# A decoder trunk: twelve output tiles of the mixer's projection by seven block products, memory's mean square in the first projections, and a triangle added behind the low keys

## The chip, the cores and the metric

The kernel runs on one core of one Trainium2 chip. The metric is the device time of one execution in microseconds, compared as a median over several runs. One further execution is recorded by the hardware profiler, and every view quoted here is of that execution.

## The reference

One layer of a decoder trunk on 512 tokens of width 2048, in float32. A mixer (12 dilated-window attention heads, 8 forgetting-attention heads, 4 heads of gated linear attention) feeds one output projection; then come cross-attention into 256 memory tokens and a gated MLP with a causal convolution of width 3. Cut to what this change touches:

```python
def reference(x, mem, ...):
    mem_n = rms_norm(mem, mem_norm)
    x = x + hybrid_mixer(rms_norm(x, norm_mix), ...)          # ends in: mixed @ w_out, 512x2048 by 2048x2048
    x = x + memory_cross_attention(rms_norm(x, norm_cross), mem_n, w_cq, w_ckv, w_co)
    x = x + conv_ffn(rms_norm(x, norm_ffn), ...)
    return rms_norm(x, norm_final)

def forgetting_attention(q, k, v, f_logit):                  # heads "b" of the mixer
    logits = q @ k.T * HEAD_DIM ** -0.5 + (c_q - c_k)         # c: running sum of log_sigmoid(f_logit)
    logits = where(kpos <= qpos, logits, -inf)                # the "triangle"
```

## The kernel before

**Precision.** Every float32 product is made of three TensorE matmuls. `split_weights` (L332 on) and `weights` (L343 on) load a block of 128 x 1024 weights into a tile `wraw` (five of them), and for each half ScalarE writes the rounded part `whi` and VectorE the rest `wlo` (five of each, 128 x 512). `mm3` (L373) then issues high by high (L375), high by low (L376) and low by high (L377).

**Activations** stand with features on the partitions: 16 tiles of 128 features by 512 tokens (`x1`, kept in `stream` tiles). A plain projection makes one output tile of 128 x 512 from 16 blocks of weights, thus 48 matmuls of 512 columns and two loads of 128 x 1024.

**Stages, in order:** first projections (`mixer`, L881 on), gated linear attention under further projections, the two groups of attention heads under their own projections (`attend`, `qk_units`), the output projection, cross-attention (`cross`), and the MLP (`up`, then down). Attention heads, gates and similar work are generators in a list `bg`; `tick` advances the first two of them between matmuls of a projection.

**The output projection** (end of `mixer`, L1012 on) has 16 tiles. The first half of the contraction of tiles 0 to 3 is issued while the last attention heads run; then come the second halves of those four, then tiles 4 to 15, one after the other, each with `weights` and `mm3` as above. `resid` adds the input tile and writes `x1`; `square` adds the squares into two tiles `sqs`, on GpSimd for even tiles and VectorE for odd ones. Under tiles 8 to 15 in program order the generator `memory` loads the memory tokens, splits them and sums their squares.

**Seven products instead of eight** exist already in the MLP. `up` takes a pair of output tiles, the two halves of the tokens and pairs of contraction tiles as a 2 x 2 block product, and makes it by the seven products of the Strassen-Winograd scheme (`product`, L1412 on: eight block pairs, thus 24 matmuls of 256 columns). The sums of weight blocks are either added on VectorE or made ahead in DRAM by accumulating DMAs from GpSimd's queue (`added`, `up_sums`, L1316); each such DMA waits for the one before on the same tile. `first_sums` and `up_sums(1)` are issued by that queue during cross-attention, `up_sums(2)` and `up_sums(3)` at the start of the attention stage. The sums of token blocks are made by ScalarE and VectorE (`token_sums`).

**Order.** A scheduler places the instructions of each engine in a static order: by program order among those whose inputs and buffers it reckons free, so a later instruction can stand ahead of one that waits. `issue_after` adds an edge that keeps an instruction behind another of the same engine. At run time each engine, and each of the DMA queues of SP, ScalarE and GpSimd, goes through its list in order.

**The triangle.** For forgetting attention, `bias_b` (L589) loads one row of running sums per head, broadcast to 128 partitions (`ba`), and adds the 128 x 128 causal mask to one block of it (L596) just ahead of the instruction that adds the bias to the scores (L546). `attend` makes the low part of the keys `kl` at L529.

Of the kernel before, what the change touches and what calls it, by code (L numbers as in the profile page):

```python
# [12 lines left out]
F32 = mybir.dt.float32  # L13
# [40 lines left out]
EARLY = 4  # L54
BELOW = 3 * PHASE
# [28 lines left out]
H0 = 4  # L84
H1 = 6
ST = 4
# [89 lines left out]
def _pack(inp):  # L176
# [26 lines left out]
    a["w_o"] = _units_out(w_out, r(D))  # L203
# [30 lines left out]
class _Trunk:  # L234
# [200 lines left out]
    def stats(self, parts, n, name, pool=None):  # L435

        nc = self.nc
        tl = n // P
        ss = self.pst("T")
        a, b = parts  # L440
        nc.vector.tensor_tensor(a, a, b, op=ALU.add)
        for t in range(tl):
            nc.tensor.matmul(ss[:, t:t + 1], a[:, t * P:(t + 1) * P], self.ones[:, 0:1], start=True, stop=True)
        rs = self.con.tile([P, tl], F32, name="rs" + name)
        nc.vector.tensor_scalar(rs, ss[:, :tl], 1.0 / D, EPS, op0=ALU.mult, op1=ALU.add)
        nc.gpsimd.tensor_tensor(rs, rs, self.mhalf[:, :tl], op=ALU.pow)

        def spread():
            bc = self.pst("T")
            for t in range(tl):  # L450
                dg = (pool or self.pre).tile([P, P], F32, name="diag", tag="diag", bufs=tl)
                nc.vector.tensor_scalar(dg, self.ident, rs[:, t:t + 1], None, op0=ALU.mult)
                nc.tensor.matmul(bc[:, t * P:(t + 1) * P], self.ones, dg, start=True, stop=True)
            big = (pool or self.con).tile([P, n], F32, name="R", tag="R", bufs=1)
            nc.scalar.activation(big, bc[:, :n], AF.Copy)
            return big

        return rs, spread
# [59 lines left out]
    def attend(self, qf, kf, e, vv, bias_of, head, mix):  # L518
# [10 lines left out]
        nc.vector.tensor_tensor(kl[a], kf[a], kh[a].bitcast(F32), op=ALU.subtract)  # L529
# [8 lines left out]
        def scores(t):  # L538
            n = P * (t + 1)
            sc = self.pst("S")  # L540
            tt = slice(t * P, n)
            with self.behind():
                nc.tensor.matmul(sc[:, :n], qs[:, tt], kh[:, :n], start=True, stop=False)
                nc.tensor.matmul(sc[:, :n], qs[:, tt], kl[:, :n], start=False, stop=True)
            pt = pts[t] = ab.tile([P, n], F32, name="pt", tag="pt", bufs=PTB, padded_shape=[P, S])
            nc.vector.tensor_tensor_reduce(pt, sc[:, :n], bias(t), -1.0, 1e38, ALU.add, ALU.min, nm[:, t:t + 1])  # L546
# [35 lines left out]
    def bias_a(self, h):  # L582
        nc = self.nc
        m = self.ab.tile([P, S], F32, name="ba", tag="ba", bufs=2)
        src = bass.AP(self.skew.tensor, self.skew.offset + h * P * GX + P - 1, [[GX - 1, P], [1, S]])
        nc.scalar.dma_start(out=m, in_=src)
        return lambda t: m[:, 384 - P * t:]

    def bias_b(self, h):  # L589
# [4 lines left out]
        def get(t):  # L594
            b = cb[:, P * t:P * (t + 1)]
            nc.vector.tensor_tensor(b, b, self.tri, op=ALU.add)  # L596
            return cb[:, :P * (t + 1)]
# [283 lines left out]
    def mixer(self):  # L881
# [63 lines left out]
        self.bg.append(self.rel_bias())  # L945
        def spread():
            with self.behind():
                self.R = self.spread()
# [31 lines left out]
        for f in range(2, EARLY):  # L980
            self.up_sums(f)
# [17 lines left out]

        def evac_o(dt):  # L1000
            def f(ps):
                self.resid(dt, ps, None, sqs, lambda n: self.mp.tile([P, n], F32, name="sqt", tag="sqt", bufs=2))
            return f
# [9 lines left out]
        units = [self.out_units(d["w_o"], n, xo, evac_o(n), box=box) for n in range(KT)]  # L1013
        self.rate = W_O / 2
        for n in range(0, 4, 2):
# [15 lines left out]
        self.flush()  # L1031
        es_ab.close()
# [12 lines left out]
        for _ in mem:  # L1045
            pass

    def memory(self):

        nc, mp = self.nc, self.mp  # L1050
        parts = [mp.tile([P, MEM], F32, name="msq%d" % i) for i in range(2)]
        self.mem = []
        for k in range(KT):
            if k % 4 == 0:
                four = mp.tile([P, 4, MEM], F32, name="mraw", tag="mraw", bufs=1)
                nc.sync.dma_start(out=four, in_=self.d["memT"][k // 4])
            raw = four[:, k % 4, :]
            hi = mp.tile([P, MEM], F32R, name="mhi%d" % k)
            lo = mp.tile([P, MEM], F32R, name="mlo%d" % k)
            self.mem.append(self.split_to(hi, lo, raw, self.gain(4, k)))  # L1060
            self.square(k, raw, parts, lambda n: mp.tile([P, n], F32, name="msqt", tag="msqt", bufs=2))
            if k % 4 == 3:
                yield
        self.mrs, spread = self.stats(parts, MEM, "m", mp)
        yield
        self.mR = spread()
        yield
# [34 lines left out]
    def cross(self):  # L1102
        nc, d, tc = self.nc, self.d, self.tc
        es = ExitStack()
        kv, mp = self.kv, self.mp
        kh, kl = {}, {}

        def evac_k(h):
            def f(ps):
                kf = mp.tile([P, MEM], F32, name="kf", tag="kf", bufs=2)  # L1110
                nc.vector.tensor_tensor(kf, ps[:, :MEM], self.mR, op=ALU.mult)
                kh[h] = kv.tile([P, MEM], F32R, name="ckh%d" % h)
                kl[h] = kv.tile([P, MEM], F32R, name="ckl%d" % h)
# [4 lines left out]
        vh = [kv.tile([P, S], F32R, name="cvh%d" % i) for i in range(MT)]  # L1118
        vl = [kv.tile([P, S], F32R, name="cvl%d" % i) for i in range(MT)]
# [12 lines left out]
        for i, u in enumerate(first):  # L1132
            more((i >= H0) + (i >= H1))
            u()
# [156 lines left out]
        s1, s5 = [self.con.tile([P, HT], F32, name=n) for n in ("s1", "s5")]  # L1291
# [20 lines left out]
    def added(self, dst, b11, b12, b22, b21):  # L1312

        def dma(i, src, **how):
            with self.tc.issue_after(self.turn.ins):
                self.turn = self.nc.gpsimd.dma_start(out=dst[i], in_=src, **how)  # L1316

        add = dict(accum_op=ALU.add, max_dma_last_dim=1024)
        dma(0, b11)
        dma(0, b12, **add)  # L1320
        dma(1, dst[0])
        dma(1, b22, **add)
        dma(2, dst[1])
        dma(2, b21, **add)
        dma(3, b12)
        dma(3, b22, **add)

    def up_sums(self, f):

        b11, b12, b22, b21 = [self.d["w_up"][4 * f + i] for i in range(4)]  # L1330
        t = [self.dr.tile([P, 1024], F32, name="up%d%d" % (f, i)) for i in range(4)]
        self.added(t, b11, b12, b22, b21)
        self.up_pre[f] = t

    def down_sums(self):
# [3 lines left out]
        for c, (p0, p1) in enumerate(FC):  # L1339
            mid = (p0 + p1) // 2  # L1340
            for k0, k1 in ((p0, mid), (mid, p1)):
# [3 lines left out]
                self.added([t[:, i * 256:(i + 1) * 256] for i in range(4)], b11, b12, b22, b21)  # L1345
                for k in range(k0, k1):
                    self.two[k] = t[(k - k0) * P:(k - k0 + 1) * P]
            for q in SUMMED[c]:
# [3 lines left out]
                self.added(t, b11, b12, b22, b21)  # L1352

    def first_sums(self):
# [13 lines left out]
        self.up_sums(1)  # L1368
# [496 lines left out]
```

## Time and profile before

| | |
|---|---|
| runs | 2251.28, 2251.34 and 5783.09 us; median 2251.34 us |
| the profiled execution | 2251.13 us, of which the span from first to last instruction is 2249.3 us |
| mean granted TensorE clock | 0.998 of full speed |
| attention stage (345 to 690 us of the span) | projections of queries, keys and values with the heads between them |
| output projection, second halves and tiles 4 to 15 | about 684 to 836.5 us |
| memory's keys and values, cross-attention | 836.5 to 988 us |
| MLP | 988 us to the end |

A page of the profile lists each engine's busy time, the queues and the costliest groups of instructions. A windows view gives, for stretches of the span, the busy time of PE (matmul), PEld (weight load), DVE (VectorE), ACT (ScalarE) and POOL (GpSimd), with the count of instructions in brackets, then the granted clock, the mean busy share of the 16 DMA engines and the GB/s that they moved. A timeline lists instructions with start, duration, engine, line and operands; "x3" means three merged into one row, and the bracket gives the idle time ahead and what ended it. Matmuls are pipelined, so their pace is read from start to start, not from their durations.

### The profile page before, as it was taken

To read this page: it belongs to the slowest core of one execution; us is meant where nothing else is said; L and a number is where in the kernel's file an instruction comes from. 1 tells how busy PE (TensorE), PEld (TensorE's weight loads), DVE (VectorE), ACT (ScalarE), POOL (GpSimd) and SP (SyncE) were. 2 spreads that over 40 slices of the span, in tenths; PEclk is the share of its full clock that TensorE was granted. 3 is DMA by queue.
4 is the path that set the end of the run, shared out by engine and by line. 5 is a ranking of instruction groups with operands and counts; after the bars stand their busy time and mean duration, and the time that the engine had idled before them with its cause. 6 is when DMAs were issued, how large, how long until landed. Compare 5 with 4: busy or idle time off the path is not lost.

```text
span 2249.3 us, 42619 instructions
## 1 busy us (share of the span) xinstructions
PE 2232.6 (99%) x15898; PEld 2089.9 (93%) x15898; DVE 1819.5 (81%) x3587; ACT 1231.7 (55%) x2532; POOL 221.3 (10%) x308
## 2 busy tenths in 40 slices
PE   9999999999999999999999999999999999999997
PEld 8898898888888888889999999999999999999997
DVE  7826756666787356699999999999999999989887
ACT  7324445555575245585555555555555575747563
POOL 2000101000002011121111111111000020101003
PEclk9999999999999999999999999999999999999999
DMA  6422157222224359589777777877534493837542
GB/s 223 162 96 82 49 150 193 97 89 99 78 92 140 122 161 241 134 206 282 198 212 201 221 208 213 215 219 224 173 132 144 145 344 104 305 124 233 186 129 82
DMA packets 141842, 377.09 MB, mean 168 GB/s; under 512 B 14484, under 2 KB 53732, under 8 KB 140932
## 3 DMA queue, kind: packets, MB, share of 16 engines
q1 hardware_dynamic: 90144, 274.18, 35.1%
q0 software_dynamic: 45728, 89.86, 18.2%
q10 hardware_dynamic: 5764, 10.35, 1.3%
q8 instruction: 124, 2.03, 0.4%
q14 instruction: 82, 0.67, 0.1%
HBM read 347.28 MB, written 91.80 MB: 195 GB/s over the span
## 4 chain that ended last, share of the span: by engine, by line
PE 96%; DVE 2%; ACT 1%; DMA 0%; issue 0%; POOL 0%; SPq 0%; DVEq 0%; ACTq 0%
PE acc L375 19%; PE acc L377 19%; PE acc L376 19%; PE psC L375 5%; PE psC L376 5%; PE psC L377 5%; PE acc L416 3%; PE acc L418 3%; PE acc L417 3%; PE psD L377 3%; PE psD L376 3%; PE psD L375 3%; PE psT L556 1%; PE psQ L377 1%; PE psQ L375 1%; PE psQ L376 1%
## 5 line engine op out<-in xcount | busy, mean ns | idle before, releaser
L336 ACT ACTIVATE whi<-wraw 128x512 fp32r<-128x512 f32 (+1 forms) x822 | 471.1, 603 | 407.3 <-PE acc L376 145.0
L337 DVE TENSOR_TENSOR wlo<-wraw,whi 128x512 fp32r<-128x512 f32 (+1 forms) x822 | 522.3, 656 | 65.9 <-ACT whi L336 61.2
L375 PE MATMUL acc<-sum,whi 128*128 128x256 f32 x1956 | 541.8, 277 | 0.4 <-ACT s L1465 0.3
L377 PE MATMUL acc<-sum,wlo 128*128 128x256 f32 x1956 | 541.5, 277 | 0.0
L376 PE MATMUL acc<-sum,whi 128*128 128x256 f32 x1956 | 541.4, 277 | 0.0
L362 DVE TENSOR_TENSOR wlo<-wraw,whi 128x512 fp32r<-128x512 f32 (+2 forms) x328 | 216.1, 665 | 191.2 <-ACT whi L361 188.8
L375 PEld LDWEIGHTS acc<-sum,whi 128*128 128x128 f32 x1956 | 367.2, 188 | 1.0 <-ACT s L1465 0.8
L377 PEld LDWEIGHTS acc<-sum,wlo 128*128 128x128 f32 x1956 | 367.3, 188 | 0.4 <-DVE wlo L337 0.2
L376 PEld LDWEIGHTS acc<-sum,whi 128*128 128x128 f32 x1956 | 367.3, 188 | 0.1
L361 ACT ACTIVATE whi<-wraw 128x512 fp32r<-128x512 f32 (+2 forms) x328 | 198.5, 610 | 284.3 <-PE acc L376 186.5
L375 PE MATMUL acc<-xhi,whi 128*128 128x512 f32 (+1 forms) x848 | 335.1, 395 | 0.5 <-ACT fg L926 0.5
L377 PE MATMUL acc<-xhi,wlo 128*128 128x512 f32 (+1 forms) x848 | 328.4, 387 | 0.0
L376 PE MATMUL acc<-xlo,whi 128*128 128x512 f32 (+1 forms) x848 | 327.9, 387 | 0.0
L375 PE MATMUL psC<-sum,whi 128*128 128x256 f32 x928 | 256.9, 277 | 0.0
L376 PE MATMUL psC<-sum,whi 128*128 128x256 f32 x928 | 256.8, 277 | 0.0
L377 PE MATMUL psC<-sum,wlo 128*128 128x256 f32 x928 | 256.5, 276 | 0.0
L377 PEld LDWEIGHTS acc<-xhi,wlo 128*128 128x128 f32 x848 | 159.3, 188 | 32.5
L375 PEld LDWEIGHTS acc<-xhi,whi 128*128 128x128 f32 x848 | 159.4, 188 | 29.9 <-ACT fg L926 0.9
L376 PEld LDWEIGHTS acc<-xlo,whi 128*128 128x128 f32 x848 | 159.7, 188 | 29.0 <-DVE xlo L324 0.2
L377 PEld LDWEIGHTS psC<-sum,wlo 128*128 128x128 f32 x928 | 174.3, 188 | 0.0
L375 PEld LDWEIGHTS psC<-sum,whi 128*128 128x128 f32 x928 | 174.3, 188 | 0.0
L376 PEld LDWEIGHTS psC<-sum,whi 128*128 128x128 f32 x928 | 174.2, 188 | 0.0
(401 smaller groups left out, 4319.0 us busy)
## 6 DMA issues: line engine op xcount, KB each, us to landing
wraw<-in_w_up SPq DMA_DIRECT2D x125, 512.0 KB, 6.3
b<-in_w_up SPq DMA_DIRECT2D x42, 512.0 KB, 4.5
wraw<-in_w_o SPq DMA_DIRECT2D x32, 512.0 KB, 3.5
wraw<-in_w_d SPq DMA_DIRECT2D x32, 448.0 KB, 4.3
wraw<-in_w_d SPq DMA_DIRECT2D x36, 384.0 KB, 5.0
wraw<-in_w_qka SPq DMA_DIRECT2D x24, 512.0 KB, 3.5
up<-in_w_up POOLq DMA_DIRECT2D x24, 512.0 KB, 7.0
one<-in_w_d POOLq DMA_DIRECT2D x24, 448.0 KB, 6.7
```

What stands on the lines that cost most here:

```text
L336: nc.scalar.activation(hi, r, AF.Copy)
L337: nc.vector.tensor_tensor(lo, r, hi.bitcast(F32), op=ALU.subtract)
L361: nc.scalar.activation(hi, r, AF.Copy)
L362: nc.vector.tensor_tensor(lo, r, hi.bitcast(F32), op=ALU.subtract)
L375: nc.tensor.matmul(out, lh, rh, start=start, stop=False, skip_group_check=more)
L376: nc.tensor.matmul(out, lh, rl, start=False, stop=False, skip_group_check=more)
L377: last = nc.tensor.matmul(out, ll, rh, start=False, stop=stop, skip_group_check=more)
L416: self.nc.tensor.matmul(o, xh[:, tt], wh, start=(k == 0), stop=False)
L417: self.nc.tensor.matmul(o, xh[:, tt], wl, start=False, stop=False)
L418: self.last = self.nc.tensor.matmul(o, xl[:, tt], wh, start=False, stop=(k == KT - 1))
L556: nc.tensor.transpose(tp[:, b * P:(b + 1) * P], pt[:, b * P:(b + 1) * P], self.ident)
```

## The change

Five things are done.

1. **Tiles 4 to 15 of the output projection** are made in three groups of four ("quads"), each of two pairs, by the seven-product scheme: per pair seven loads of 128 x 1024 and seven times 24 matmuls of 256 columns. Tiles 0 to 3 stay plain; all four are now evacuated after the last of them. The two pairs of a quad alternate; quads 0 and 1 take the products in the order 1, 2, 4, 5, 6, 3, 7 and the last one in the order 5, 6, 3, 7, 1, 2, 4. A pair's closing sums (`ends`) and its additions to the input (`out`) are issued between the products of the next quad, or of the same one in the last quad.
2. **The sums of weight blocks** are made in DRAM ahead of time (`out_sums`): two groups of three pairs, eight accumulating or copying steps each, every step cut into two DMAs of 384 x 512 elements (768 KB), thus 32 DMAs on GpSimd's queue at the start of the attention stage, ahead of `up_sums` for 2, 3 and now also 1.
3. **The sums of token blocks** for products 5, 6, 3 and 7 are made by a generator `token_turns` on VectorE and ScalarE: four steps before the fourth plain tile, the others between the products of quad 0.
4. **Memory**: its mean square moves to the background work of the first projections (`mem_stats`, with its own loads of the memory tokens); the splitting stays in the output projection, two tiles after each of eight products in the last quad, into the buffers that the token sums leave. The spread of the mean square over 128 partitions follows in cross-attention, and the splits of `x1` (H0, H1) and the root (ST) start later by one or two units there.
5. **The triangle** is added by an instruction that is placed behind the low part of the keys.

Squares of tiles 4 to 15 are now added by VectorE alone. `first_sums` is placed behind `pooled`, which is now an instruction of VectorE.

```diff
-H0 = 4
-H1 = 6
-ST = 4
+PLAIN = 4
+QUADS = (KT - PLAIN) // 4
+LAST_ORDER = (5, 6, 3, 7, 1, 2, 4)
+OUT_ORDER = (1, 2, 4, 5, 6, 3, 7)
+H0 = 6
+H1 = 7
+ST = 6
...
-        for n in range(4):
-            units[n][1]()
-        mem = self.memory()
-        for n in range(4, KT):
-            for u in units[n]:
-                u()
-                if n >= M0:
-                    next(mem, None)
+        for n in range(PLAIN):
+            w = self.weights(d["w_o"][2 * n + 1])
+            for kk in range(8):
+                wh, wl = w(kk * P, P)
+                self.mm3(box[n], wh, wl, *xo[8 + kk], False, kk == 7)
+            if n == PLAIN - 2:
+                turns = self.token_turns([self.mix[m] for m in order], xo)
+                for _ in range(4):
+                    next(turns)
+        for n in range(PLAIN):
+            evac_o(n)(box[n])
+        for c in range(QUADS):
+            last = c == QUADS - 1
+            if last:
+                next(mem)
+            self.quad(PLAIN + 4 * c, LAST_ORDER if last else OUT_ORDER, mem if last else turns,
+                      c == QUADS - 2)
...
+    def token_turns(self, raw, xo):
...
+        def split(j, v):
+            th, tl = [tok[j, v, n] for n in range(2)]
+            src = a[v].rearrange("p i c -> p (i c)")
+            nc.scalar.activation(th, src, AF.Copy)
+            tt(tl, src, th.bitcast(F32), ALU.subtract)
+        def part(j, v):
+            k = 4 * v
+            if j == 5:
+                a[v] = temp()
+                pair(a[v], lambda i: (raw[k + 2 * i + 1][:, hi], raw[k + 2 * i][:, hi]), ALU.subtract)
...
+    def quad(self, d0, order, steps, swap):
...
+        def out(o, i):
+            dt = o["d"] + i
+            t = o["gp" if i else "val"]
+            x1 = self.x1[dt] = self.stream(dt)
+            raw = self.wp.tile([P, S], F32, name="xraw", tag="wraw", bufs=WR, padded_shape=[P, 1024])
+            nc.sync.dma_start(out=raw, in_=self.d["xT"][dt // 2, :, dt % 2, :])
+            tt(x1, raw, t, ALU.subtract if i else ALU.add)
+            nc.scalar.activation(t, x1, AF.Square)
+            self.pooled = tt(self.sqs[i], self.sqs[i], t, ALU.add)
...
+        for n, j in enumerate(order):
+            for o in pairs:
+                s1, s5 = o["s1"], o["s5"]
+                parts = self.halves(self.up_raw(o["src"][j]))
+                for _ in range(2 if early and n == 0 else 1):
+                    if todo:
+                        todo.popleft()()
+                ps = bank(o, where[j])
+                for i in range(NP):
+                    th, tl = parts[i // 4]
+                    c = slice(i % 4 * P, (i % 4 + 1) * P)
+                    self.mm3(ps, th[:, c], tl[:, c], *self.operand(j, i), i == 0 and j not in (2, 3, 7),
+                             i == NP - 1, more=True)
...
-        def get(t):
+        def get(t, after):
             b = cb[:, P * t:P * (t + 1)]
-            nc.vector.tensor_tensor(b, b, self.tri, op=ALU.add)
+            with self.tc.issue_after(after.ins):
+                nc.vector.tensor_tensor(b, b, self.tri, op=ALU.add)
...
-        for f in range(2, EARLY):
+        self.out_sums()
+        for f in (2, 3, 1):
             self.up_sums(f)
...
+    def mem_stats(self):
+        for k in range(0, KT, 2):
+            raw = self.mc.tile([P, 2, MEM], F32, name="mraw", tag="str", bufs=6)
+            nc.sync.dma_start(out=raw, in_=self.d["memT"][k // 4, :, k % 4:k % 4 + 2, :])
...
+    def out_sums(self):
+        w, n = self.d["w_p"], (KT - PLAIN) // 4
+        for g in range(2):
+            t = [self.dr.tile([n * P, 1024], F32, name="wo%d%d" % (g, i)) for i in range(4)]
+            b11, _, b22, b21 = b = [w[i, g * n:(g + 1) * n].rearrange("k p c -> (k p) c") for i in range(4)]
+            cuts = [slice(512 * h, 512 * (h + 1)) for h in range(2)]
+            self.added(*[[[x[:, c] for c in cuts] for x in y] for y in (t, b)])
```

More of the change, by code (lines that the diff above doesn't have):

```diff
@@ L1012, in mixer @@
         xo, box = Lazy(), {}
-        units = [self.out_units(d["w_o"], n, xo, evac_o(n), box=box) for n in range(KT)]
         self.rate = W_O / 2
-        for n in range(0, 4, 2):
+        for n in range(0, PLAIN, 2):
             raws = []
@@ L1036, in mixer @@
         self.mp = self.pool(self.es_mp, "mp", "right")
[L1037 to L1051 removed]
+        self.todo = deque()
+        mem = self.mem_steps = self.memory()
@@ L1052, in memory, with load @@
+    def memory(self):
+        nc = self.nc
+        def load(k):
+            two = self.spare([P, 2, MEM])
+            nc.sync.dma_start(out=two, in_=self.d["memT"][k // 4, :, k % 4:k % 4 + 2, :])
+            return two
+        loads = [load(0), load(2)]
         self.mem = []
+        yield
         for k in range(KT):
-            if k % 4 == 0:
-                four = mp.tile([P, 4, MEM], F32, name="mraw", tag="mraw", bufs=1)
-                nc.sync.dma_start(out=four, in_=self.d["memT"][k // 4])
@@ L1057, in memory @@
[L1057 to L1062, printed above, removed]
+            if k % 2 == 0:
+                two = loads.pop(0)
+            both = self.ring()
+            self.mem.append(self.split_to(both[:, :MEM], both[:, MEM:], two[:, k % 2, :], self.gain(4, k)))
@@ L1063, in memory @@
+            if k % 2:
+                if k + 3 < KT:
+                    loads.append(load(k + 3))
                 yield
-        self.mrs, spread = self.stats(parts, MEM, "m", mp)
+        self.mR = self.mspread()
         yield
-        self.mR = spread()
+    def mem_stats(self):
+        nc = self.nc
+        both, temps = [self.con.tile([P, S], F32, name="sq%d" % i, tag="sq%d" % i) for i in range(2)]
+        parts, temps = [[t[:, :MEM], t[:, MEM:]] for t in (both, temps)]
+        self.rsm = self.con.tile([P, MT], F32, name="rsm")
+        for k in range(0, KT, 2):
+            raw = self.mc.tile([P, 2, MEM], F32, name="mraw", tag="str", bufs=6)
+            nc.sync.dma_start(out=raw, in_=self.d["memT"][k // 4, :, k % 4:k % 4 + 2, :])
+            for i in range(2):
+                sq = temps[i] if k else parts[i]
+                nc.scalar.activation(sq, raw[:, i, :], AF.Square)
+                if k:
+                    nc.vector.tensor_tensor(parts[i], parts[i], sq, op=ALU.add)
+            yield
+        with self.behind():
+            self.mrs, self.mspread = self.stats(parts, MEM, "m", lambda shape: self.low(shape[1], F32))
@@ L1133, in cross @@
             more((i >= H0) + (i >= H1))
+            if i == 2:
+                next(self.mem_rest)
+                ready.append(True)
+                for f, ps in keys:
+                    f(ps)
             u()
```

192 lines of the change are left out of this document (159 added, 33 removed).

## The prediction

> **What bounds the kernel.** I read the page first: how busy PE is, and which engine the chain that ended last runs through.
>
> ```profile
> span 2249.3 us, 42619 instructions
> PE 2232.6 (99%) x15898; PEld 2089.9 (93%) x15898; DVE 1819.5 (81%) x3587; ACT 1231.7 (55%) x2532; POOL 221.3 (10%) x308
> ...
> PE 96%; DVE 2%; ACT 1%; DMA 0%; issue 0%; POOL 0%; SPq 0%; DVEq 0%; ACTq 0%
> ```
>
> The chain is PE for 96% of the span: an instruction less on PE is time saved, and work on another engine costs only where it makes PE wait. So the windows view comes next, for the stages that the change touches: first projections, start of the attention stage, its middle with the forgetting heads, output projection (tiles 4 to 15 as they stand now), memory's keys, and a stretch of the MLP that already works with seven products.
>
> ```profile
> 45.00:180.00 135.00, 134.96 (x693) 122.15 (x692) 75.59 (x129) 48.12 (x89) 5.04 (x9) 1.00 0.36 126
> 307.70:390.00 82.30, 82.08 (x410) 70.26 (x409) 53.57 (x130) 45.65 (x101) 12.56 (x17) 1.00 0.73 192
> 560.00:635.00 75.00, 74.63 (x365) 61.21 (x364) 53.46 (x147) 43.30 (x98) 0.00 (x0) 1.00 0.26 92
> 705.40:836.50 131.10, 131.10 (x584) 108.70 (x583) 59.58 (x95) 50.32 (x90) 15.64 (x17) 1.00 0.42 141
> 836.50:862.00 25.50, 25.50 (x206) 24.96 (x205) 22.31 (x39) 17.62 (x31) 2.07 (x2) 1.00 0.99 263
> 1147.20:1166.30 19.10, 19.10 (x170) 19.10 (x169) 18.65 (x31) 10.55 (x20) 2.00 (x3) 1.00 0.71 199
> ```
>
> The reader should see that PE has no gap in the projection, where DVE is busy for less than half the time, and none in the MLP either, where DVE is busy for 18.65 of 19.10 us. Seven products can thus keep PE full beside a DVE at 98%. Next is what one matmul costs, from start to start, in timelines: evacuations of two successive plain tiles, and the same ScalarE copy in two successive steps of the MLP.
>
> ```profile
> 738.04 0.69 DVE L1073 TENSOR_TENSOR str<-acc,xraw 128x512 f32<-128x512 f32 x1 [1.53 <-PE acc L377]
> 748.92 0.69 DVE L1073 TENSOR_TENSOR str<-acc,xraw 128x512 f32<-128x512 f32 x1 [1.53 <-PE acc L377]
> ...
> 1128.06 0.39 ACT L1465 ACTIVATE s<-acc 128x256 f32<-128x256 f32 x1 [0.81 <-PE acc L377]
> 1147.18 0.39 ACT L1465 ACTIVATE s<-acc 128x256 f32<-128x256 f32 x1 [0.81 <-PE acc L377]
> ```
>
> A plain tile takes 10.88 us for 48 matmuls, 0.2267 us for 512 columns. A step of the MLP takes 19.12 us for 7 x 24, 0.1138 us for 256. Half the columns cost half the time, so seven products are really seven eighths.
>
> **Tiles 4 to 15.** Removed: 12 x 48 = 576 matmuls at 0.2267, 130.6 us. Added: 3 quads x 14 products x 24 = 1008 at 0.1138, 114.7 us. On PE that is **-15.9 us**, and PE is the path.
>
> What must fit beside it, per quad of 14 x 2.73 = 38.2 us, is two splits per product, token sums or memory's splits, and evacuations. DVE decides; its pitch is shorter than its durations:
>
> ```profile
> 1156.62 0.41 DVE L1435 TENSOR_TENSOR u<-s,acc 128x256 f32<-128x256 f32 x1
> 1156.95 1.89 DVE L337 TENSOR_TENSOR wlo<-wraw,whi 128x512 fp32r<-128x512 f32 x3
> 1158.76 0.42 DVE L1435 TENSOR_TENSOR gp<-psC,u 128x256 f32<-128x256 f32 x1
> ```
>
> 256 columns cost 0.33 (1156.62 to 1156.95), 512 columns 0.60 (1.81 for three). Quad 0: 28 splits 16.8; nine parts of token sums, each two of 256 and one of 512, 11.3; three sums for product 7 and four placements of two each, 4.6; its own evacuation 4 x 0.33 = 1.3; plain tiles, five of 512, 3.0: together 37.0. Quad 1: 16.8, closing sums 2.0, four outputs of two each 4.8, own 1.3: 24.9. Quad 2: 16.8, what quad 1 leaves 6.8, own 3.3, two outputs 2.4, and memory's 16 splits at about 0.40 (an estimate between the two pitches) 6.4: 35.7. All are below 38.2, the first two closely. ScalarE has less: 28 roundings at 0.63 and, in quad 0, nine of 0.63, eight of 0.41 and six of 0.38 make 28.9.
>
> ```profile
> L361 ACT ACTIVATE whi<-wraw 128x512 fp32r<-128x512 f32 x264 | 165.3, 629 | 215.9 <-PE acc L376 174.7 <-PE acc L418 28.8 <-issue 4.6
> L1604 ACT ACTIVATE sum<-graw 128x256 fp32r<-128x256 f32 x83 | 29.1, 407 | 1.7 <-DMA graw<-gd 1.7
> L1465 ACT ACTIVATE s<-acc 128x256 f32<-128x256 f32 x42 | 16.1, 383 | 30.5 <-PE acc L377 30.5
> ```
>
> The four early token steps, at most 4 x 1.26 = 5.0 us, lie under the plain tiles. PE's loss in the quads lies between nothing (the MLP row) and, if DVE's 37.0 and 35.7 were stretched to durations of 0.42 and 0.69, 44.1 - 38.2 and 42.3 - 38.2, together 10.0. I take **+1.5**, half a microsecond a quad, since the MLP is the same code on a fuller DVE. SP's queue carries 42 loads of 512 KB in 115 us, 192 GB/s, about what it moves in the MLP row (199); it adds twelve loads of input tiles and eight of memory, and loads of sums wait for GpSimd's queue (below).
>
> **Sums of weight blocks.** 32 DMAs of 768 KB stand ahead of 24 of 512 KB on GpSimd's queue, which is in order. Its timeline now, first and last of 16 issues, with one that has two in flight, and the first square after them:
>
> ```profile
> 307.74 0.61 POOL L1316 DMA_DIRECT2D up<-in_w_up  x1
> ...
> 337.26 1.55 POOL L1316 DMA_DIRECT2D up<-in_w_up  x2 [3.45 <-DMA up<-up]
> 346.81 1.52 POOL L1316 DMA_DIRECT2D up<-in_w_up  x2 [8.00 <-DMA up<-in_w_up]
> ...
> 388.23 1.02 POOL L1316 DMA_DIRECT2D up<-in_w_up  x1 [6.86 <-DMA up<-in_w_up]
> 691.67 1.42 POOL L1090 TENSOR_TENSOR sq<-str 128x512 f32<-128x512 f32 x1 [302.42 <-DVE str L1073]
> ```
>
> 80.5 us for 15 DMAs is 5.4 each, 98 GB/s; two in flight move 1 MB in 9.55 us, 110 GB/s. At these the 32 take 8.1 or 7.2 us each, 258 or 229 us, and end at 566 or 537; the 24 add 129 and end at 695 or 666. The first sum is needed near 705.4 + 4 x 2.73 = 716, the second group's near 760: **0**. The far end is a row of sums cut finely, 512 KB in 8.7 us:
>
> ```profile
> two<-in_w_d POOLq DMA_DIRECT2D x12, 512.0 KB, 8.7
> ```
>
> That would be 13 us each one after the other, 418 us, the sums ready at 726 and the queue free at 855; this end is the second rival. The traffic falls where the DMA share was 0.73 with the same kind of sums and PE lost 0.22 of 82.3 us; I put no more on it. `up_sums(1)`, gone from cross-attention, takes load off the stretch with a share of 0.99: nothing, as PE is full there.
>
> **Memory.** The squares leave, the splits stay:
>
> ```profile
> L329 DVE SCALAR_TENSOR_TENSOR mlo<-mraw,gains,mhi 128x256 fp32r<-128x256 f32 x16 | 12.0, 770 | 7.7 <-ACT mhi L328 7.7
> L1094 ACT ACTIVATE msqt<-mraw 128x256 f32<-128x256 f32 x14 | 5.6, 402 | 0.0
> L1096 DVE TENSOR_TENSOR msq<-msq,msqt 128x256 f32<-128x256 f32 x7 | 3.7, 533 | 0.0
> L443 PE MATMUL psT<-ones,msq 128*128 128x1 f32 x4 | 0.5, 229 | 0.0
> ```
>
> In the first projections 16 squares of 0.40 and 15 additions of at most 0.53 make 6.4 us of ScalarE and 8.0 of DVE, beside 87 and 59 us in which they idle between 45 and 180 us; the cover gone, that would be up to 14. SP gets eight loads of 256 KB more, at a DMA share of 0.36. PE's matmuls for it only move. **0.** In cross-attention the splits of `x1` begin two units later, but DVE no longer has the sums there; 22.31 of 25.50 us are busy now, and four outputs (4.8 us) come over from quad 2 into 16 units of 2.73: **0**.
>
> **Triangle.** What DVE waits for before it, and the wait that the chain shows:
>
> ```profile
> L596 DVE TENSOR_TENSOR ba<-ba,tri 128x128 f32<-128x128 f32 x32 | 9.0, 284 | 3.9 <-DMA ba<-cdr 3.8
> 588.39 4.19 DMA ba<-cdr
> ```
>
> The add no longer stands ahead of the low keys while the row lands. Between 0 and the 3.8 us that DVE loses; PE idles only 0.37 us in that window: **-0.3**. Behind the add stand only instructions that need it.
>
> **Sum.** 2251.13 (the profiled execution, 0.2 below the median of the runs) - 15.9 + 1.5 - 0.3 = 2236.4; on the median **2236.6 us**.
>
> **A rule against the rows.** The Trainium skill ("TensorE: Matmul & The Clock Gate", section "Wait — 56ns, not 53.3ns?") puts a warm matmul at its columns over 2.4 GHz plus about 2.5 ns from start to start, an estimate of 215.8 ns for 512 and 109.2 for 256. By that rule the fixed part is paid twice and the exchange is 124.3 - 110.1, -14.2 us, which would give 2238.3. The trace's 226.7 and 113.8 ns show no such fixed part, at a granted clock of 1.00, and decide.
>
> **Rivals.** *A, the quads are bound by DVE.* For it: 37.0 of 38.2 us leave little when token sums, splits and evacuations bunch. Against it: the MLP row. With the 10.0 from above in place of 1.5: 2245.1.
>
> *B, slower: squares wait behind the sums.* GpSimd still squares plain tiles 0 and 1, and DVE's addition for tile 3 needs the second of these near 707 us. Let the queue end its sums at E: GpSimd needs two squares of 1.42, DVE waits until E + 2.9, and with it every split behind that addition. PE has about five halves of split weights in hand, 6.8 us, so it starves from E = 711 on. My E is 666 to 695, so this is near; it sets in above 8.6 us per DMA. At E = 726 the gain is gone; at 772 the kernel is 2% slower; at 855 it stands at 2236.6 + 144 = 2381. For it: the 8.7 us row. Against it: those are rows of 1 KB, and the squares may have been placed ahead of the last sums. The Trainium skill ("SBUF — State Buffer", section "Who interferes with whom") names a cause that would slow this queue: a DMA issued from GpSimd cannot have its descriptors written while DVE holds the port that they share. No row here shows it: with DVE busy for 53.57 of 82.30 us the sums still went out every 5.4.
>
> *C, 256 columns are not half.* Memory's keys run such matmuls, too, with the smaller tiles that they read:
>
> ```profile
> 836.67 0.28 PE L375 MATMUL acc<-mhi,whi 128*128 128x256 f32 x1
> ...
> 837.02 0.28 PE L375 MATMUL acc<-mhi,whi 128*128 128x256 f32 x1
> ```
>
> 0.1167 us: 1008 of them cost 117.6, the gain is 13.0 and the time 2239.5. Against it: the long MLP stretch at 0.1138.
>
> **How the numbers follow.** Forecast 0.62, A 0.13, B 0.17, C 0.08. The forecast's own range is 2234.5 (no loss in the quads) to 2240. Half of B lies below 2250. The range 2234 to 2249 takes in A, C and that half; left out are 0.09 above and some 0.05 below. About 2%, 45 us, is what a measurement of this kernel can tell from no change. Faster than that would need three times PE's saving: 0.01. Slower needs E above 772: 0.03. The rest, 0.96, is within it.
>
> **What the profile will show.** Right: 128x256 matmuls of the output projection at 0.114 us, the quads from about 705 to 821 us, PE full there, GpSimd's last sum before about 700, everything after earlier by 15 us. Wrong: DVE at 100% with PE idle before products 5, 6 or 3 (A); GpSimd's squares after 711 and a gap of PE behind them (B); SP waiting for a sum, or heads of the attention stage losing time to the added traffic, which I priced at nothing.

## The result, and the profile after

The changed kernel takes 2276.83 us in the median (2274.68 to 2280.19), the kernel before 2251.34 on the same chip: a ratio of 1.011, 95% interval 1.010 to 1.012. Of six executions of the kernel before, one took 5783.09 us and is left out of the median. The changed kernel is slower by 25.5 us, where 14.7 us less were forecast, and 28 us above the upper end of the range.

The page of the changed kernel, its first lines and the chain that ended last:

```profile
span 2272.9 us, 43844 instructions
...
PE 92%; DVE 3%; issue 2%; ACT 2%; DMA 1%; POOL 0%; DVEq 0%; SPq 0%; ACTq 0%; POOLq 0%
```

PE had 96% of the chain before. The windows of the stages, which have moved by up to 37 us (start, first projections, first heads, quads, memory's keys):

```profile
0.00:45.00 45.00, 35.72 (x163) 34.03 (x163) 23.39 (x39) 23.94 (x43) 8.53 (x18) 0.89 0.87 251
45.00:180.00 135.00, 114.01 (x547) 100.16 (x548) 83.25 (x154) 49.93 (x105) 17.73 (x29) 0.91 0.50 154
742.20:860.70 118.50, 118.50 (x1009) 118.50 (x1008) 99.13 (x187) 78.62 (x153) 3.30 (x1) 1.00 0.66 217
860.70:873.00 12.30, 12.30 (x108) 12.30 (x107) 12.29 (x22) 10.37 (x20) 0.00 (x0) 1.00 0.82 296
344.70:427.00 82.30, 82.07 (x410) 70.25 (x409) 54.38 (x130) 45.61 (x101) 17.31 (x15) 1.00 0.89 222
```

The quads are as foreseen: PE without a gap, DVE at 99.13 of 118.50 us (37.0 + 24.9 + 35.7 = 97.6 were reckoned). The loss stands in the first two rows, in stages for which the prediction named only memory's squares: PE is busy for 35.72 of 45 and 114.01 of 135 us, and its granted clock is 0.89 and 0.91. The timeline from the first scores of the attention stage on shows the same: they begin at 382.18 us, before at 345.17. So 37.0 us are lost ahead of the attention stage; from the last product of the heads to the first transposition of cross-attention the changed kernel takes 198.45 us (723.91 to 922.36), before 211.00 (687.05 to 898.05), a gain of 12.55. The rest moves by less than a microsecond.

The chain of the changed kernel in order of time (start, length, what), its pieces of the first 80 us:

```profile
2.37 7.46 DMA pre<-in_w_up
9.82 10.09 issue
19.91 1.05 POOL pre L1599
20.96 10.04 issue
31.00 1.01 POOL pre L1599
...
49.72 1.03 POOL pre L1599
50.98 6.05 DMA str<-in_xT
64.51 9.45 DMA mraw<-in_memT
```

`pre` are the sums of `first_sums`, which SP reads from 968 us on in the kernel before. They stood at 829 to 893 us there. Now GpSimd issues them first of all, and the kernel's start hangs on them. How, is in the timeline (SPq is SP's DMA queue):

```profile
27.10 0.42 SPq L357 DMA_DIRECT2D wraw<-in_w_first  x1
...
49.72 1.03 POOL L1599 DMA_DIRECT2D pre<-in_w_up  x1 [5.05 <-issue]
50.35 0.60 POOL L924 COPY mark<-str 128x1 f32<-128x1 f32 x1
...
50.98 0.80 SPq L915 DMA_DIRECT2D str<-in_xT  x2
57.05 0.72 ACT L335 ACTIVATE xhi<-str,gains 128x512 fp32r<-128x512 f32 x1 [21.70 <-DMA str<-in_xT]
...
59.43 0.71 PE L423 MATMUL acc<-whi,xhi 128*128 128x408 f32 x1 [17.37 <-ACT whi L368]
77.83 0.80 PE L382 MATMUL acc<-xhi,whi 128*128 128x512 f32 x1 [6.56 <-ACT fg L934]
```

Read it upwards from PE. PE stands for 17.37 us, for a rounding of weights that follows in ScalarE's order on an input tile; SP asks for this tile at 50.98, and it lands at 57.03. SP asked for nothing after 27.10, as the six buffers of `str` were taken. Its list of waits says for whom (us in all, times, longest):

```profile
SPq L915 <- POOL mark L924: 21.4, 1, 21.4
```

The oldest buffer is read by the copy `mark<-str` on GpSimd, and this copy, which needs nothing but that tile, is behind the sums in GpSimd's order and runs at 50.35; in the kernel before it ran at 16.09. A queue that PE never waits for held back a copy of one column, that a buffer, that SP, and that PE.

Why the sums went there: `first_sums` is placed behind `self.pooled`. Before, that was an addition on GpSimd; the quads now set it to an addition on VectorE, and a mark on another engine gave the sums no place in GpSimd's order: in the third experiment, which has no edge at all, they stand at the same times. The line is in `quad`: `self.pooled = tt(...)`. The section on the change names the new mark in its last sentence, but neither it nor the prediction asks what that does to GpSimd's order.

### The profile page after: what moved, and what is told of

The parts are those of the page before. It is cut to its first block, busy times and chain, and to the rows that moved or that the text cites. A ratio compares the mean times of both kernels' runs of the same rounds, so it can differ in the third digit from the quotient of the medians.

```text
span 2272.9 us, 43844 instructions
## 1 busy us (share of the span) xinstructions
PE 2228.2 (98%) x16330; PEld 2106.5 (93%) x16330; DVE 1874.2 (82%) x3718; ACT 1267.0 (56%) x2610; POOL 250.1 (11%) x325
## 4 chain that ended last, share of the span: by engine, by line
PE 92%; DVE 3%; issue 2%; ACT 2%; DMA 1%; POOL 0%; DVEq 0%; SPq 0%; ACTq 0%; POOLq 0%
PE acc L382 17%; PE acc L384 17%; PE acc L383 17%; PE psC L382 5%; PE psC L383 5%; PE psC L384 5%; PE psD L382 3%; PE psD L384 3%; PE psD L383 3%; PE acc L423 2%; PE acc L425 2%; PE acc L424 2%; PE psT L563 1%; PE psQ L384 1%; PE psQ L382 1%
## 5 line engine op out<-in xcount | busy, mean ns | idle before, releaser
L343 ACT ACTIVATE whi<-wraw 128x512 fp32r<-128x512 f32 (+2 forms) x906 | 523.3, 605 | 442.3 <-PE acc L383 157.9
L344 DVE TENSOR_TENSOR wlo<-wraw,whi 128x512 fp32r<-128x512 f32 (+2 forms) x906 | 579.6, 658 | 83.5 <-ACT whi L343 77.8
L369 DVE TENSOR_TENSOR wlo<-wraw,whi 128x512 fp32r<-128x512 f32 (+2 forms) x280 | 182.2, 658 | 163.9 <-ACT whi L368 162.0
L382 PE MATMUL acc<-xhi,whi 128*128 128x512 f32 (+1 forms) x800 | 301.9, 378 | 6.6 <-ACT fg L934 6.6
L384 PE MATMUL acc<-xhi,wlo 128*128 128x512 f32 (+1 forms) x800 | 295.1, 369 | 0.0
L383 PE MATMUL acc<-xlo,whi 128*128 128x512 f32 (+1 forms) x800 | 294.8, 369 | 0.0
L368 ACT ACTIVATE whi<-wraw 128x512 fp32r<-128x512 f32 (+2 forms) x280 | 168.1, 606 | 206.4 <-PE acc L383 110.9
L382 PEld LDWEIGHTS acc<-xhi,whi 128*128 128x128 f32 x800 | 151.1, 189 | 28.9 <-ACT fg L934 6.9
L384 PEld LDWEIGHTS acc<-xhi,wlo 128*128 128x128 f32 x800 | 151.0, 189 | 25.4
L383 PEld LDWEIGHTS acc<-xlo,whi 128*128 128x128 f32 x800 | 151.3, 189 | 21.6 <-DVE xlo L331 0.3
```

Of the source, the lines that this page charges most:

```text
L343: nc.scalar.activation(hi, r, AF.Copy)
L344: nc.vector.tensor_tensor(lo, r, hi.bitcast(F32), op=ALU.subtract)
L368: nc.scalar.activation(hi, r, AF.Copy)
L369: nc.vector.tensor_tensor(lo, r, hi.bitcast(F32), op=ALU.subtract)
L382: nc.tensor.matmul(out, lh, rh, start=start, stop=False, skip_group_check=more)
L383: nc.tensor.matmul(out, lh, rl, start=False, stop=False, skip_group_check=more)
```

## The experiments

**Theory:** the lost place of `first_sums` is the whole loss, by GpSimd's order. **Rivals:** the traffic of the sums on the DMA engines; memory's squares in the first projections, which fill the 6.56 us at 77.83; the new parts of the change themselves.

### The sums behind the last sum of the up blocks

```
-        with self.tc.issue_after(self.pooled.ins):
+        with self.tc.issue_after(self.turn.ins):
```

> The changed kernel, with the eleven DMAs of first_sums placed behind the last of the up sums on GpSimd's own queue (after about 680 us) instead of at its head. Queue theory: at the head of the queue they hold up the copy of x tile 8, and with it SP's loads; the 17.4 us gap of PE at 42 us and the two of 2.9 us at 6 and 11 us go, and the clock loss with them, 26 to 30 us in all: about 2248. Rival, memory's mean square alone makes the loss: no change, 2275 to 2277. The wait at the end of the first projection (6.6 us in the changed kernel) stays under both.

Measured: 2243.23 us, ratio 0.9956 (0.9941 to 0.9971). The sums ran from 638 to 692 us. PE's wait of 17.37 us is gone, and the one of 6.56 is this row:

```profile
43.69 0.50 PE L382 MATMUL acc<-xhi,whi 128*128 128x512 f32 x1 [1.40 <-ACT fg L934]
```

One edge turns 25 us of loss into 9 us of gain, 5 us more than I expected: I had left the wait of 6.56 us as it was, and it goes too. What it needs besides the delay is in the run with memory's squares later.

### The sums behind the mark, still at the start

```
+        with self.tc.issue_after(self.begun.ins):
```

> The changed kernel, with first_sums placed just behind the copy of x tile 8 and the small constant loads, but ahead of the inverse root of the first mean square (rsx) on GpSimd's queue. Queue theory: the gap at 42 us goes, since SP's loads no longer wait for the copy; instead rsx comes behind about seven accumulating DMAs of 5 to 10 us that start near 22 us, so PE waits at the end of the first projection, from about 44 until 70 to 80 us; the total is 2270 to 2290. Rival, it is the traffic on the shared DMA engines that starves the loads: no single gap of that kind, the loss spread and about half of that of the changed kernel, near 2262.

Measured: 2272.36 us, ratio 1.0081 (1.0064 to 1.0097). The timeline:

```profile
56.49 1.47 POOL L453 TENSOR_TENSOR rsx<-rsx,mhalf 128x4 f32<-128x4 f32 x1
61.18 0.79 PE L382 MATMUL acc<-xhi,whi 128*128 128x512 f32 x1 [18.30 <-ACT fg L934]
...
76.64 1.12 POOL L661 COPY fg<-fg 128x64 f32<-128x64 f32 x4
77.82 1.10 PE L671 MATMUL psT<-ident,fg 128*112 128x128 f32 x4 [8.12 <-POOL fg L661]
```

The copy runs at 16.48, and SP's stream of input tiles no longer stops: PE runs through to 42.9 us. The wait has gone to the next two things that GpSimd has to do between sums, the power for the mean square (`rsx`, ahead of the 18.30 us) and the gates' copy (`fg`, 8.12). VectorE had the input of `rsx` ready at 47.06; GpSimd took it up at 56.49, behind the sum that it issued at 55.76. That is the order of the queue.

It doesn't clear the traffic, though, since the sums start at 26.96 here, when SP has asked for the last input tile (22.8). For the first two waits of the changed kernel traffic is the likelier cause: ScalarE waits for the input tiles themselves, and SP's only wait for the copy comes later.

```profile
9.40 0.48 PE L423 MATMUL acc<-whi,xhi 128*128 128x408 f32 x1 [2.77 <-ACT xhi L335]
13.88 0.71 PE L423 MATMUL acc<-whi,xhi 128*128 128x408 f32 x1 [2.57 <-ACT xhi L335]
```

The input tiles take longer to land (last number, median in us) in the changed kernel, second, than in the kernel before, first, and in this run, third:

```profile
str<-in_xT SPq DMA_DIRECT2D x15, 256.0 KB, 5.2
str<-in_xT SPq DMA_DIRECT2D x15, 256.0 KB, 9.0
str<-in_xT SPq DMA_DIRECT2D x15, 256.0 KB, 5.5
```

No run separates traffic from order for these two waits; both come from the same misplaced sums.

### The kernel before with its first sums set free

```
-        with self.tc.issue_after(self.pooled.ins):
+        with ExitStack():
```

> The kernel before with one edit: first_sums has no edge, so it and up_sums(1), which follows it, can stand at the head of GpSimd's queue. Queue theory: the loss appears without any other part of the change: a gap of 15 to 20 us before x tile 14, and a second one behind rsx; 2270 to 2300. Rival, the loss needs memory's mean square or the new weight sums: at most 5 us, below 2257.

Measured: 2296.11 us, ratio 1.0194 (1.0178 to 1.0209), with these waits in the timeline of PE:

```profile
59.76 0.71 PE L416 MATMUL acc<-whi,xhi 128*128 128x408 f32 x1 [17.72 <-ACT whi L361]
85.12 0.79 PE L375 MATMUL acc<-xhi,whi 128*128 128x512 f32 x1 [13.84 <-ACT fg L926]
```

No other part of the change is in it, neither quads nor memory's squares, and the loss is there: 44 us, and 45.0 are lost ahead of the attention stage (its first scores begin at 390.15). That is more than the 37.0 of the changed kernel, because `up_sums(1)` stands behind the first sums here: its DMAs run from 65 us on, and `rsx` waits among them until 80.83.

### Memory's squares later

The squares on ScalarE are placed behind the last evacuation of the first projection (`fg`); the sums stay at the start.

> The changed kernel, with memory's squares placed on ScalarE behind the last evacuation of the first projection. Theory: VectorE and ScalarE hold rsx and the evacuations up behind memory's squares, which wait for their loads; the 6.6 us wait of PE near 71 us shrinks to 1 or 2, the gap at 42 us stays: about 2271. Rival, that wait belongs to the late queue too (rsx itself is late): no change, 2275 to 2277.

Measured: 2278.46 us, ratio 1.0115 (1.0100 to 1.0130): no gain. The wait of 6.56 us shrinks to 0.50, and these come in its place:

```profile
112.19 0.80 PE L382 MATMUL acc<-xhi,whi 128*128 128x512 f32 x1 [3.60 <-ACT whi L368]
114.51 0.79 PE L384 MATMUL acc<-xhi,wlo 128*128 128x512 f32 x1 [1.09 <-DVE wlo L369]
...
130.78 0.61 PE L450 MATMUL psT<-ones,sq 128*128 128x1 f32 x4 [1.27 <-DVE sq L448]
```

My expectation missed: bunched later, the same squares hold up the splits of weights. For the 6.56 us it takes both, the late start and the squares: the wait falls to 1.40 us without the one and to 0.50 without the other. What the squares cost by themselves is the next run.

### Without memory's squares

14 of the 16 squares leave, with their additions; the sums stand behind the up blocks:

```
-            for i in range(2):
+            for i in range(0 if k else 2):
                 sq = temps[i] if k else parts[i]
```

> The changed kernel with the weight-block sums behind the first projection, and with 14 of the 16 squares of the memory and their 15 additions left out; the loads stay, and the mean square is that of two tiles alone. The prediction priced these squares at 0. At the end of the first projection PE stands 1.40 us in the run with them, 0.68 in the kernel before. If the squares cost there, the gap falls to about 0.7 and the time from 2243.2 to about 2242.4; if they had cost as much as the 6.6 us seen at that place in the changed kernel, the time would fall to 2237. Rival: the squares are covered wholly, and the time stays within 0.5 us of 2243.2.

Measured: 2243.28 us, ratio 0.9959 (0.9946 to 0.9971), the same time as with them. At the end of the first projection PE's starts show an excess of 0.69 us, as in the kernel before (0.68), where the five runs that have the squares and an undisturbed start show 1.6 to 2.5. So the squares cost 0.9 to 1.8 us at that place. In the total it can't be seen, since this run lost 1.73 us at 632 us to a late bias row (below).

### The triangle, alone and undone

> The kernel before with only the triangle's add moved behind the low keys. The prediction's step gave -0.3 us, from 0.37 us in which PE idles there. Theory: DVE's 3.8 us of waiting for the bias row shrinks by at most one instruction of 0.4 us a head, and the time stays within 0.5 us of 2252. Rival: the add delays a split behind it, and the time rises by 1 us or more.

Measured, on the kernel before: 2251.56 against 2251.82 us, ratio 0.9999 (0.9990 to 1.0008). And undone, beside the sums behind the up blocks:

> The changed kernel with the weight-block sums behind the first projection, and with the triangle's add back where it was, ahead of the low keys. In the run with the new place, DVE waited 7.9 us in five heads for the bias row, and PE stood 1.16, 1.15 and 0.82 us at 597, 633 and 671 us. Theory: the row lands later (6.3 us in the median against 3.7 before) because the sums for the output projection run beside it on the DMA engines, and which instruction DVE stands in does not matter much; then the waits stay near 8 us, PE's three gaps stay near 3 us together, within 1 us, and the time stays within 1.5 us of 2243. Rival: the new place is what costs, as the add now stands ahead of a weight split; then the three gaps go, and the time falls by 2.5 to 3 us.

Measured: 2245.95 us, ratio 0.9972 (0.9960 to 0.9984), gaps of 1.32 and 1.20 us at 598 and 634 still there. Together the gaps are within the expectation; VectorE's waits for the row (11.4 us in six heads, not near 8) and the time (2.7 us above the run with the new place, not within 1.5) are not. The executions range from 2241.96 to 2249.75, and the intervals of the two runs overlap, so the place of the triangle's add makes no difference that can be told here; the rival, in which the time falls without the new place, fails.

### What the sums do to the heads

In the run with the sums behind the up blocks, PE's starts show 1.16, 1.15 and 0.82 us lost in three heads. The timeline shows DVE held by a bias row, and PE by DVE:

```profile
597.06 0.29 DVE L604 TENSOR_TENSOR ba<-ba,tri 128x128 f32<-128x128 f32 x1 [1.61 <-DMA ba<-cdr]
...
598.21 0.51 PE L583 MATMUL psO<-ptl,vv 128*128 128x512 f32 x1 [1.00 <-DVE ptl L572]
```

These runs move sums away from the heads. First the `first_sums` alone, with the mark left on GpSimd, where it was before:

```
-            self.pooled = tt(self.sqs[i], self.sqs[i], t, ALU.add)
+            tt(self.sqs[i], self.sqs[i], t, ALU.add)
```

> The changed kernel with one word less: the additions on VectorE in the quads no longer set the mark that the first sums of the MLP stand behind, so that they stand behind the last square sum on GpSimd, near 710 us, as in the kernel before. In the run with these sums behind the last sum of the up blocks, they ran from 638 to 693 us, beside the last heads. Theory: the start runs as in that run, without the 18 and the 29 us of the changed kernel; and the gap of 0.82 us at 671 us, in the heads, goes with them, so the time is 0.5 to 1 us below 2243.2, about 2242.5, or 9 to 10 us below the kernel before. Rival: beside the quads the sums hold up the loads of their weights, PE has gaps between 712 and 790 us, and the time is 2245 or more.

Measured: 2240.58 us, ratio 0.9953 (0.9940 to 0.9965), the sums at 710 to 783 us. This is the lowest median: one word less, and 36 us off the changed kernel. It is 2 us below the expectation, and by the intervals it can't be told from the run with the sums behind the up blocks (0.9956). The rival falls: PE has no gap in the quads, at a DMA share of 0.88:

```profile
707.20:825.80 118.60, 118.60 (x1010) 118.56 (x1009) 99.16 (x187) 78.57 (x153) 12.54 (x12) 1.00 0.88 265
```

Then the sums of the up blocks as well:

> As the run with the first sums behind the last square sum, and with the 24 sums of the up blocks 2, 3 and 1 taken from the heads to the same place, ahead of the first sums, so that no sums run from about 510 to 710 us. Theory: the bias rows of the heads land late because these sums share the DMA engines with them; then they land in about 3.7 us in the median as in the kernel before (6.3 with the sums), VectorE waits for them 4 us in all in place of 7.9, the gaps at 597, 633 and 671 us fall below 0.5 us each, and the time is 2 to 2.5 us less than with the sums, about 2240. Rival: the rows land late for another reason, and the gaps and the time stay. What could hide the gain: the sums now share the DMA engines with the quads' loads and with cross-attention's, where the share was 0.7 to 0.99.

Measured: 2243.34 us, ratio 0.9966 (0.9955 to 0.9978). The rows of the list of DMAs for the bias row, which end in the median time from issue to landing in us; the kernel before first,

```profile
ba<-cdr ACTq DMA_DIRECT2D x8, 256.0 KB, 3.7
```

then the sums behind the up blocks,

```profile
ba<-cdr ACTq DMA_DIRECT2D x8, 256.0 KB, 6.3
```

and this run:

```profile
ba<-cdr ACTq DMA_DIRECT2D x8, 256.0 KB, 4.0
```

So the traffic of the sums does delay the bias rows, by some 2 us. Whether PE pays for it differs from run to run: the run with only `first_sums` moved kept the up blocks' sums there, landed in 5.8 us, and lost nothing at 597, 633 and 671 us. And part of what the last run gains in the heads it gives back at the start of cross-attention, where the sums now share the DMA engines: PE waits 1.03 and 0.55 us near 849 us. The 2240 us that I expected didn't come.

### The pace of 256 columns

The quads take 118.55 us in place of 114.7, without a gap. Four rows of PE's timeline of the changed kernel, first matmuls of products; from 764.98 to 770.44 lie 48 matmuls, from 775.94 to 793.22 lie 144:

```profile
764.98 0.28 PE L382 MATMUL acc<-tok,whi 128*128 128x256 f32 x1
770.44 0.28 PE L382 MATMUL psC<-tok,whi 128*128 128x256 f32 x1
775.94 0.28 PE L382 MATMUL acc<-xhi,whi 128*128 128x256 f32 x1
793.22 0.29 PE L382 MATMUL psC<-xhi,whi 128*128 128x256 f32 x1
```

Token sums `tok` go at 0.1138 us each, the input tiles `xhi` and `xlo` at 0.1200. By the addresses in the program these tiles begin 192 bytes past a multiple of 256, `tok` 128, the weights 192. The edit moves `xhi` and `xlo` by 64 bytes, to 128:

```
-        edge.tile([P, 8], F32, name="edge")
+        edge.tile([P, 8 + PHASE], F32, name="edge")
...
-        self.kv.tile([P, PHASE], F32, name="ledge")
```

> The changed kernel with the weight-block sums behind the first projection, and beside that the 128x512 tiles xhi and xlo moved by 64 bytes in memory; no instruction is added or taken away. In the run before it, with xhi and xlo at 192 bytes past a multiple of 256 like the weights, products 1, 2, 4 and 7 of the quads ran at 120 ns per 256-column matmul, and products 5, 6 and 3, which read tok at 128, at 114. If the address of the moving tile sets the pace, the 576 matmuls on xhi and xlo fall to 114 ns each: 576 x 6 ns = 3.5 us less, a quad takes 38.3 us in place of 39.5, and the time is about 2239.7 us against 2243.2. The rival, that the pace hangs on the kind of tile (how it is written, which engine, or that two tiles alternate) and not on its address, gives 120 ns and 2243.2 again.

Measured: 2291.57 us, ratio 1.0175 (1.0161 to 1.0189). The same 144 matmuls of the second quad now run from 748.06 to 764.39, 0.1134 each:

```profile
748.06 0.28 PE L382 MATMUL acc<-xhi,whi 128*128 128x256 f32 x1
764.39 0.28 PE L382 MATMUL psC<-xhi,whi 128*128 128x256 f32 x1
```

The address theory holds there, and yet the kernel is 48 us slower. By the addresses of the two programs the shift also moved most of the MLP's sums from 128 to 64, which I hadn't seen, and the plain 512-column products went from 0.2267 to 0.2333 us. A step of the MLP, between two copies of the same line, takes 19.92 us in place of the 19.12 of before:

```profile
1126.66 0.38 ACT L1696 ACTIVATE s<-acc 128x256 f32<-128x256 f32 x1 [0.86 <-PE acc L384]
1146.58 0.39 ACT L1696 ACTIVATE s<-acc 128x256 f32<-128x256 f32 x1 [0.86 <-PE acc L384]
```

So the address theory holds for the quads, and the total goes the other way. The last run measures the pace by itself.

> Matmuls alone: everything else of the kernel is left out. 128x512 and 128x256 moving tiles of the type of the kernel's, in the kernel's order of three (hi with the high weights, lo with the high weights, hi with the low weights), 72 for each pair of places, where the moving tile begins 0, 64, 128 or 192 bytes past a multiple of 256 (ma, mb, mc, md) and the weights likewise (wa, wb, wc, wd); all pairs once forwards, then once backwards. Theory: the two addresses alone set the pace. Then both passes agree pair by pair, 256 columns take 120 ns with both at 192 and 113 with the moving tile at 128 and the weights at 192, and 512 columns take 227 with both at 192 and 233 with 128 and 192, as in the run with the shifted tiles. Rival: the pace is a state of the stream of matmuls that outlasts the pair, so that the two passes differ for the same pair, or that it comes from what other engines do to the memory, so that all pairs take 113 and 227.

Worked out from the starts of PE's rows, 72 matmuls a pair, with the place of the moving tile less that of the weights, modulo 256 bytes:

| moving less weights | 512 columns, ns | 256 columns, ns |
|---|---|---|
| 0 | 226.8 to 227.4 | 119.7 to 120.0 |
| 64 | 229.0 to 229.2 | 117.7 to 117.8 |
| 128 | 232.3 to 232.5 | 118.5 to 118.7 |
| 192 | 233.2 to 233.3 | 113.3 to 113.7, and 117.7 to 117.8 in two of eight |

How it is read, on the first matmuls of four pairs (`mb`, `mc`, `md`, `ma` are 64, 128, 192 and 0, weights `wc` 128):

```profile
365.08 0.28 PE L280 MATMUL near<-mbhi,wchi 128*128 128x256 f32 x1
373.26 0.28 PE L280 MATMUL near<-mchi,wchi 128*128 128x256 f32 x1
381.88 0.28 PE L280 MATMUL near<-mdhi,wchi 128*128 128x256 f32 x1
390.37 0.28 PE L280 MATMUL near<-mahi,wdhi 128*128 128x256 f32 x1
```

The pair 64 and 128 takes 8.18 us, 113.6 ns each; 128 and 128, 8.62 us, 119.7; 192 and 128, 8.49 us, 117.8. The difference of the two addresses sets the pace, whatever they are, and no other engine works here. Both passes agree but for two pairs, 0 with weights at 64 and 192 with weights at 0, which run at 113.6 or 113.7 in one pass and at 117.7 or 117.8 in the other. In each pass these two follow one another, and the later one is the slow one: there the rival, a state of the stream, has its part. The shifted run shows that too, with whole products on `tok`, whose addresses hadn't moved, at 0.1178 (731.51 to 733.63, 18 matmuls). Otherwise the table gives what that run measured: its input tiles stand 192 from the weights (113.4 and 233.3), and the MLP's sums, at 64, stand 128 from them (19.92 us for 168 matmuls is 118.6).

So `xhi` and `xlo`, at the weights' own place, stand best for 512 columns and worst for 256: the plain tiles had the good case, and the quads read the same tiles in the bad one.

## Why the prediction failed

**The step that failed is the placing of `first_sums`.** The change part by part has no term for it: it counts GpSimd's queue from 307 us on, with 32 and 24 DMAs, and leaves out the 11 that the changed mark set loose. The section on the change names the new mark, and the prediction puts it at nothing without a reason. Priced by comparison of the changed kernel with its one-word variant, the term is 2276.83 - 2240.58 = 36.2 us. Rival B has the same mechanism, GpSimd's order holding other engines up, but it isn't what happened: B put it at the squares near 707 us. In the run that put `first_sums` behind the other sums, the last of all was issued at 692 us and the squares began at 699: B's threshold of 711 wasn't reached.

**Of the 37.0 us, not all is waiting.** PE's waits of 2.77, 2.57, 17.37 and 6.56 us, less the 0.51 of before, make 28.8. The first two, 5.34 us, are the ones for which traffic is the likelier cause; the long one is GpSimd's order; the last needs the late start and memory's squares together. The other 8.2 are matmuls at a lower clock behind the waits. In the windows of the changed kernel, up to, right behind and after the long wait:

```profile
0.00:59.40 59.40, 35.72 (x163) 34.03 (x163) 23.39 (x39) 26.28 (x48) 14.95 (x30) 0.81 0.86 235
59.43:64.00 4.57, 4.57 (x13) 4.14 (x14) 4.57 (x8) 2.48 (x5) 3.64 (x6) 0.50 1.04 313
64.00:70.90 6.90, 6.90 (x41) 6.89 (x40) 2.78 (x7) 2.50 (x8) 0.00 (x0) 0.98 1.10 291
```

13 matmuls start in 4.57 us at a granted clock of 0.50, then 41 in 6.90 at 0.98. The clock is 0.50 from 10 to 16 us as well and 0.78 from 16 to 25, and 0.58 from 78 to 82. With the busy time of PE these clocks cost 3.8, 2.4 and 1.8 us behind the first two waits, the long one and the last: 8.0 of the 8.2. The Trainium skill ("TensorE: Matmul & The Clock Gate", section "Part 1: The HAM clock gate (the "warmup" mystery)") says that the clock halves after an idle window of about 3.4 us and comes back after as long a busy one; the row of the long wait agrees in kind, with 4.9 us from 59.43 to the return of the clock. Behind the waits of 2.77 and 2.57 us, shorter than such a window, the clock was at 0.50 too; there the measurement decides.

**Tiles 4 to 15, -15.9 + 1.5:** right in kind. 576 of the 1008 matmuls read input tiles and took 0.1200 in place of 0.1138: 576 x 0.0062 = 3.6 us more. PE lost nothing for the 1.5 reckoned. -15.9 + 3.6 = -12.3, against -12.55 between the two events. Rival C came near the size (0.1167, a gain of 13.0 us) by luck: its tiles, memory's keys, begin at 128 like `tok`, 192 from the weights, where the matmuls run at 113.6 or at 117.8, while the input tiles of the quads begin at the weights' own place and run at 120.0. It isn't the columns but the place of the operands. Rival A is wrong; DVE at 99.13 of 118.50 us fits the sum made for it.

**Sums of weight blocks, 0:** right for the quads, whose 32 DMAs were done long before. For the heads it was low: bias rows land 2 us later, which costs 0 to 3 us, depending on the run. The prediction named it as what would prove it wrong, and it did so a little.

**Memory, 0:** low by 0.9 to 1.8 us. The place that was looked at, 45 to 180 us with 87 and 59 us idle, isn't the one that pays; that is the evacuation at 42 to 45 us, where PE already waited for ScalarE. Beside the late start they cost more, as part of the 6.56 us.

**Triangle, -0.3:** can't be told from 0 (interval -2.3 to +1.8 us).

With the one word taken out the kernel is at 2240.58 us: the forecast of 2236.6 plus 3.6 for the pace, less 1.5, plus about 1.8 for memory gives 2240.5. These terms were chosen after the runs, and the measurement's interval, 2238 to 2244, can't confirm the last microsecond of it.

## What to carry to other kernels

When a value that marks an order changes its engine, look for everyone who waits for it, and find where each of them stands in the new order of its own engine, from the first instruction on; an edge that loses its effect stands on an unchanged line, and shows in no diff. A queue that the bound engine never waits for can still stop it, if it holds one short instruction that frees a buffer. And a pace read from one tile holds for its place against the weights: compare rows of the same tiles.

## What the runs showed of the hardware

For this kernel's operands a matmul's pace hangs on where its two operands lie to each other: 226.8 to 233.3 ns for 512 columns and 113.3 to 120.0 for 256, with the best place for the one being the worst for the other. The Trainium skill ("TensorE: Matmul & The Clock Gate", section "Wait — 56ns, not 53.3ns?") gives one pace for each width, from which 215.8 and 109.2 ns follow as an estimate; the measurements differ and decide. A shift of many of its tiles by 64 bytes cost this kernel 48 us (2291.57 against 2243.23). What makes one pairing run at 113.6 or at 117.8 ns stays open; no run here separates it.
